# Prefix sums along the diagonal of four matrices: summing the upper part in one running row per partition, and loading the last full group row by row

## The chip, the cores and the metric

One core of one Trainium2 chip. The span is the time from the first to the last instruction in one profiled execution; it is about 1.7 us shorter than the time. TensorE is PE in the profile (PEld: its weight loads), VectorE is DVE, ScalarE is ACT, GpSimd is POOL, and SyncE, which issues the loads here, is SP.

## The reference

```python
B, H, W = 4, 4224, 4224
def reference(x):                       # x: fp32 [B, H, W]
    ps = np.cumsum(np.cumsum(x, axis=1), axis=2)
    diag = np.diagonal(ps, axis1=1, axis2=2)
    return np.cumsum(diag, axis=1).astype(np.float32)
```

Only the diagonal of the two-dimensional prefix sum is wanted, but every element of x has a part in it. So all of x, 285 MB, must be read once, and the output is 66 KB.

## The kernel before

Rows come in strips: a group is 384 rows, three per partition (F = 3), loaded whole as a [128, 3, 4224] tile (6336 KB) into one of three buffers. An image has 11 such groups. The step from diagonal element i-1 to i adds row i up to the diagonal and column i above it. So, per group, the kernel needs row sums to the left of the diagonal (ScalarE for 5/8 of the columns, VectorE for the rest; an instruction that sums a row also writes a by-product, a copy of what it summed: 128x2144 for 128x2144 in ScalarE's sums of group 8) and column sums to the right of it (VectorE adds the three rows of a partition, TensorE adds over the 128 partitions by multiplying with a selector). The block on the diagonal is split by a triangular mask.

```python
def add_up(strip, g, ws):                     # one group of 384 rows, before (shortened)
    k, hi = row_of(g), (g + 1) * GW
    mu = mup.tile([P, F, GW], FP32, name="mu")
    for q in range(F):
        act_sum(acc[:, k, q, 0:1], strip[:, q, :ws])             # ScalarE, writes a dump tile
    for q in range(F):
        masked(mu[:, q, :], strip[:, q, g*GW:hi], um3[:, q, :], acc[:, k, q, 2:3])
    for q in range(1, F):
        add_to(mu[:, 0, :], mu[:, q, :])
    columns(g, mu[:, 0, :], minus_sel)                           # TensorE
    if hi < N:
        for q in range(1, F):
            add_to(strip[:, 0, hi:], strip[:, q, hi:])
        for j in range(g + 1, NG):
            columns(j, strip[:, 0, j*GW:(j+1)*GW])               # TensorE, up to ten of them
    for q in range(F):
        pair_sum(acc[:, k, q, 1:2], strip[:, q, ws:hi])          # VectorE
```

The last image ends otherwise. Its group 10 comes in small pieces (called the last pieces below: two pieces of two thirds of the rows, five of the rest), and behind them stands a chain: row sums of d (`pu`), the carry between groups on TensorE, two scans, the weighing of the last sums, two small stores. Here d is the tile in which TensorE collects the steps along the diagonal (one row per group), and r3 are the row sums, which TensorE adds into d in six passes.

## Time and profile before

| | before |
|---|---|
| time, median of 3 (all of them) | 677.53 us (676.79 to 678.2) |
| span of the profiled execution | 675.7 us |
| busy: PE, DVE, ACT | 281.8, 387.9, 198.0 us |
| passes on PE, instructions on DVE | 576, 738 |
| read from memory | 285.47 MB |
| group 8 of the last image lands | 640.6 us |
| group 9 of the last image lands | 655.7 us |
| row sums of d (`pu`) start | 663.9 us |

How to read it: a landing is seen as the start of the first ScalarE operation on a strip, which waits for the load. The page's rows of tenths and of GB/s cut the span into 40 slices of 16.9 us; the timeline lists instructions in order with their start, their duration and, in brackets, the idle time before them and what ended it. The lines of both stand in the prediction.

### The profile page before, as it was taken

The page shows a single profiled execution, that of the slowest core. Times are in us where ns is not written, and L with a number is a line of the kernel's source. Part 1 is how long each engine was busy: PE and PEld are TensorE (multiplying, and loading weights), DVE is VectorE, ACT ScalarE, POOL GpSimd, SP SyncE. Part 2 cuts the span into 40 slices and gives each one's busy share as a digit, 9 for nine tenths or more (in the row PEclk, how much of TensorE's full clock was granted, in tenths as well). Part 3 has the DMA queues.
Part 4 walks back from the last instruction along what each step waited for, and adds up shares of the span by engine and source line. Part 5 has one row for each costly group of instructions (what it writes and reads, how often), then busy time and mean ns, then how long its engine had stood idle before and what let it go on. Part 6 is the DMA issues. An engine that isn't in the chain of part 4 may idle for free.

```text
span 675.7 us, 2520 instructions
## 1 busy us (share of the span) xinstructions
PE 281.8 (42%) x576; PEld 70.3 (10%) x576; DVE 387.9 (57%) x738; ACT 198.0 (29%) x275; POOL 7.1 (1%) x30
## 2 busy tenths in 40 slices
PE   0366455521037644532105545543212555663224
PEld 0021111100002111100001111100000111110002
DVE  1678666443377766444347776544445777554556
ACT  0121322334412122233451112223453111222446
POOL 4000000000000000000000000000000000000000
PEclk9977766665557777755556877775655687766666
DMA  9999999999999999999999999999999999999993
GB/s 384 432 419 433 432 432 433 438 439 430 432 432 432 435 436 432 433 432 432 432 435 432 432 433 431 432 432 432 432 432 436 432 432 433 432 432 430 435 400 128
DMA packets 7938, 285.69 MB, mean 423 GB/s; under 512 B 840, under 2 KB 1396, under 8 KB 2164
## 3 DMA queue, kind: packets, MB, share of 16 engines
q1 hardware_dynamic: 7924, 285.55, 98.2%
q8 instruction: 4, 0.07, 0.0%
q14 instruction: 10, 0.08, 0.0%
HBM read 285.47 MB, written 0.07 MB: 423 GB/s over the span
## 4 chain that ended last, share of the span: by engine, by line
DMA 72%; DVE 13%; PE 11%; ACT 2%; issue 1%; SPq 0%; DVEq 0%; ACTq 0%
DMA strip<-in_x_dram 72%; PE d L207 10%; DVE strip L236 8%; DVE mu L239 2%; ACT dump L214 2%; DVE mu L236 2%; PE fin_b L207 0%; DVE pair L225 0%; DVE c L377 0%; PE fin_a L207 0%; SPq L69 0%; DVE c L239 0%; DVE pu L219 0%; DVE yl L416 0%; DVE r L219 0%
## 5 line engine op out<-in xcount | busy, mean ns | idle before, releaser
L214 ACT ACTIVATE dump<-strip 128x224 bf16<-128x224 f32 (+13 forms) x137 | 184.0, 1343 | 453.4 <-DMA strip<-in_x_dram 450.4
L207 PE MATMUL d<-strip,sel 128*33 128x384 f32 (+1 forms) x440 | 223.3, 677 | 130.6 <-DVE strip L236 130.6
L239 DVE SCALAR_TENSOR_TENSOR mu<-strip,um 128x384 f32<-128x384 f32 x129 | 65.2, 555 | 265.0 <-DMA strip<-in_x_dram 265.0
L236 DVE TENSOR_TENSOR strip<-strip 128x3840 f32<-128x3840 f32 (+9 forms) x80 | 188.4, 2355 | 1.4
L207 PE MATMUL d<-mu,minus_sel 128*33 128x384 f32 (+1 forms) x86 | 51.9, 698 | 249.6 <-DVE mu L236 249.6
L207 PEld LDWEIGHTS d<-strip,sel 128*33 128x33 f32 (+1 forms) x440 | 58.2, 140 | 301.6 <-DVE strip L236 170.5
L225 DVE SCALAR_TENSOR_TENSOR pair<-strip 128x80 bf16<-128x80 f32 (+12 forms) x138 | 81.7, 592 | 3.2
L236 DVE TENSOR_TENSOR mu<-mu 128x384 f32<-128x384 f32 x86 | 47.8, 556 | 1.5
L207 PEld LDWEIGHTS d<-mu,minus_sel 128*33 128x33 f32 (+1 forms) x86 | 7.2, 122 | 283.9 <-DVE mu L236 280.9
L214 ACT ACTIVATION_READ_ACCUMULATOR dump<-strip 128x1 f32 x137 | 25.5, 186 | 0.0
L225 DVE DVE_READ_ACCUMULATOR pair<-strip 128x1 f32 x138 | 11.3, 82 | 0.0
L239 DVE DVE_READ_ACCUMULATOR mu<-strip,um 128x1 f32 x129 | 10.7, 83 | 0.0
L214 ACT ACT_TABLE_LOAD x1 | 1.3, 1283 | 19.1 <-DMA strip<-in_x_dram 19.1
L207 PE MATMUL d<-ones_all,r 128*33 128x128 f32 (+1 forms) x12 | 2.3, 346 | 5.9 <-DVE r L219 5.9
L200 DVE TENSOR_SCALAR steps<-steps 128x128 int32<-128x128 int32 x1 | 0.5, 461 | 5.8 <-POOL steps L199 5.8
L207 PE MATMUL fin_a<-weights,arows 128*1 128x256 f32 (+1 forms) x4 | 1.4, 513 | 3.1 <-DVE arows L219 3.1
L207 PEld LDWEIGHTS d<-ones_all,r 128*33 128x33 f32 (+1 forms) x12 | 1.4, 132 | 8.7 <-issue 5.3
L219 DVE TENSOR_REDUCE r<-acc 128x99 f32<-128x297 f32 (+1 forms) x2 | 0.7, 360 | 2.6 <-ACT dump L214 2.6
L207 PE MATMUL fin_b<-weights,bsum 128*1 128x128 f32 (+2 forms) x12 | 2.1, 364 | 0.0
L377 DVE TENSOR_TENSOR_SCAN c<-ones_all,carry,c 33x384 f32<-33x384 f32 (+1 forms) x2 | 2.0, 1008 | 0.1
L102 DVE MEMSET um<- 128x1152 bf16 (+1 forms) x2 | 1.4, 698 | 1.1 <-PEq L465 1.1
L377 DVE TENSOR_TENSOR_SCAN c<-ones_all,carry,d 33x384 f32<-33x384 f32 (+1 forms) x2 | 2.0, 1002 | 0.1
(62 smaller groups left out, 23.8 us busy)
## 6 DMA issues: line engine op xcount, KB each, us to landing
strip<-in_x_dram SPq DMA_DIRECT2D x43, 6336.0 KB, 32.1
strip<-in_x_dram SPq DMA_DIRECT2D x1, 2304.0 KB
strip<-in_x_dram SPq DMA_DIRECT2D x1, 1536.0 KB
strip<-in_x_dram SPq DMA_DIRECT2D x3, 480.0 KB, 31.4
head<-in_x_dram SPq DMA_DIRECT2D x1, 576.0 KB
strip<-in_x_dram SPq DMA_DIRECT2D x1, 352.0 KB, 32.0
strip<-in_x_dram SPq DMA_DIRECT2D x1, 128.0 KB, 24.7
out_dram<-c SPq DMA_DIRECT2D x1, 49.5 KB
```

What stands on the lines that cost most here:

```text
L102: nc.vector.memset(um, -1.0)
L200: nc.vector.tensor_single_scalar(out=steps, in_=steps, scalar=2, op=ALU.arith_shift_right)
L207: nc.tensor.matmul(o, lhsT=lhsT, rhs=rhs, start=start, stop=False, skip_group_check=True)
L214: nc.scalar.activation(out=dump[:, :w], in_=src, func=ACT.Copy, accum_out=acc)
L219: nc.vector.reduce_sum(out=acc, in_=src, axis=AX.X)
L225: nc.vector.scalar_tensor_tensor(out=pair[:, :w], in0=src[:, :w], scalar=1.0, in1=src[:, w:], op0=ALU.mult, op1=ALU.add, accum_out=acc,)
L236: nc.vector.tensor_add(out=o, in0=o, in1=i)
L239: nc.vector.scalar_tensor_tensor(out=o, in0=i, scalar=1.0, in1=m, op0=ALU.mult, op1=ALU.mult, accum_out=acc,)
L377: nc.vector.tensor_tensor_scan(out=c12[:, i, :], data0=ones_row[:rows], data1=src, initial=carry[:, i : i + 1], op0=ALU.mult, op1=ALU.add,)
```

## The change

The intent is to relieve TensorE and the start of each buffer's next load: VectorE adds everything on and above the diagonal up in one fp32 row u per partition, over all groups of an image, and TensorE reads a block of u once, when the group reaches it. ScalarE sums the full rows to the left, and writes its by-product into the strip itself instead of a dump tile. The head (the block on the diagonal of the last group) is loaded first, and group 9 of the last image is loaded and summed row by row.

```diff
-            add_up(strip, g, hi * 5 // 8 // 32 * 32)
+            for q in range(F):
+                act_sum(rsum[:, k, q : q + 1], strip[:, q, :hi])
+            block = strip[:, :, lo:hi]
+            nc.vector.tensor_mul(out=block, in0=block, in1=um3)
+            row_sums(rabove[:, k, :], block)
+            if g == 0:
+                nc.vector.tensor_add(out=u, in0=strip[:, 0, :], in1=strip[:, 1, :])
+                add_to(u, strip[:, 2, :])
+            else:
+                for q in range(F):
+                    add_to(u[:, lo:], strip[:, q, lo:])
+            columns(g, u_of(g))
 ... (in the last image, for g = 9)
+            for q in range(F):
+                load(out=strip[:, q, :], in_=rows_of(b, g)[:, q, :])
+            for q in range(F):
+                act_sum(rsum[:, k, q : q + 1], strip[:, q, :wa])         # wa = 2304
+                pair_sum(more[:, q : q + 1], strip[:, q, wa:hi])
+                block = strip[:, q, lo:hi]
+                masked(block, block, um3[:, q, :], rabove[:, k, q : q + 1])
+                add_to(u[:, lo:], strip[:, q, lo:])
+            for j in (g, LG):
+                columns(j, u_of(j))
+            add_to(rsum[:, k, :], more)
 ... (ScalarE's sum)
-        nc.scalar.activation(out=dump[:, :w], in_=src, func=ACT.Copy, accum_out=acc)
+        nc.scalar.activation(out=src, in_=src, func=ACT.Copy, accum_out=acc)
 ... (sums of the first of the last pieces: from before pu to after the carry's matmuls)
-            sum_a(1, *acuts[0], acuts[0][0] + 1536)
+        if not whole:
+            sum_a(1, *acuts[0], acuts[0][0] + 1536)
```

More of the change, by code (lines that the diff above doesn't have):

```diff
@@ L51 @@
     strips = ctx.enter_context(tc.tile_pool(name="strips", bufs=NBUF))
-    mup = ctx.enter_context(tc.tile_pool(name="mup", bufs=1))
     dumpool = ctx.enter_context(tc.tile_pool(name="dump", bufs=1))
@@ L63 @@
     ctx.enter_context(tc.manual_schedule())
-    def strip_tile():
-        return strips.tile([P, F, N], FP32, name="strip")
-    def load_rows(o, b, r0):
-        nc.sync.dma_start(
-            out=o, in_=x[b, r0 : r0 + GW, :].rearrange("(p f) w -> p f w", f=F)
-        )
-    prefetched = []
-    for i in range(NBUF):
-        t = strip_tile()
-        load_rows(t, 0, i * GW)
-        prefetched.append(t)
     NH = N - GW
@@ L85, with strip_tile, rows_of @@
     nc.sync.dma_start(out=head, in_=src[:, :, NH:N])
-    def selector(name, value):
-        t = consts.tile([P, 2 * NW - 1], FP32, name=name)
-        nc.vector.memset(t, 0.0)
-        nc.vector.memset(t[:, NW - 1 : NW], value)
-        return t
+    def strip_tile():
+        return strips.tile([P, F, N], FP32, name="strip")
+    def rows_of(b, g):
+        return x[b, g * GW : (g + 1) * GW, :].rearrange("(p f) w -> p f w", f=F)
+    load = nc.sync.dma_start
+    prefetched = []
+    for i in range(NBUF):
+        t = strip_tile()
+        load(out=t, in_=rows_of(0, i))
+        prefetched.append(t)
+    sel = consts.tile([P, 2 * NW - 1], FP32, name="sel")
+    nc.vector.memset(sel, 0.0)
+    nc.vector.memset(sel[:, NW - 1 : NW], 1.0)
     um3 = consts.tile([P, F, GW], BF16, name="um3")
@@ L98 @@
     for um, pattern, cm in (
+        (um1, [[1, GW]], -1),
         (um3, [[-1, F], [1, GW]], -F),
-        (um1, [[1, GW]], -1),
     ):
-        nc.vector.memset(um, -1.0)
+        nc.vector.memset(um, 1.0)
         nc.gpsimd.affine_select(
@@ L111 @@
         )
-    sel = selector("sel", 1.0)
-    minus_sel = selector("minus_sel", -1.0)
     ones_all = consts.tile([P, P + GW], FP32, name="ones_all")
@@ L211, in act_sum @@
     def act_sum(acc, src):
-        w = src.shape[-1]
-        dump = dumpool.tile([P, 2688], BF16, name="dump")
-        nc.scalar.activation(
-            out=dump[:, :w], in_=src, func=ACT.Copy, accum_out=acc
-        )
+        nc.scalar.activation(out=src, in_=src, func=ACT.Copy, accum_out=acc)
     def row_sums(acc, src):
@@ L223, in pair_sum @@
         w = src.shape[-1] // 2
-        pair = dumpool.tile([P, 1024], BF16, name="pair")
+        pair = dumpool.tile([P, 768], FP32, name="pair")
         nc.vector.scalar_tensor_tensor(
@@ L247, in masked @@
         )
-    accs = []
+    sums, above = [], []
     for i, n in enumerate((NW, NG)):
-        accs.append(consts.tile([P, n, F, 3], FP32, name=f"acc{i}"))
-        nc.gpsimd.memset(accs[i], 0.0)
+        for tiles, name in ((sums, "sums"), (above, "above")):
+            tiles.append(consts.tile([P, n, F], FP32, name=f"{name}{i}"))
+    for t in (sums[1], above[1]):
+        nc.vector.memset(t[:, 0, :], 0.0)
     asum = last.tile([P, 2, 5], FP32, name="asum")
@@ L260 @@
     hu = last.tile([P, 3], FP32, name="hu")
-    hmu = last.tile([P, F, GW], FP32, name="hmu")
-    def do_head():
-        row_sums(hs, head)
-        for h in range(F):
-            w = GW - h * P
-            masked(
-                hmu[:, h, GW - w :], head[:, h, GW - w :], um1[:, :w], hu[:, h : h + 1]
-            )
-        for h in range(1, F):
-            add_to(hmu[:, 0, h * P :], hmu[:, h, h * P :])
-        nc.vector.tensor_add(out=dtot, in0=hs, in1=hu)
-        nc.vector.tensor_copy(out=asum[:, :, 0], in_=dtot[:, 0:2])
+    row_sums(hs, head)
+    for h in range(F):
+        t = head[:, h, h * P :]
+        masked(t, t, um1[:, : GW - h * P], hu[:, h : h + 1])
+    for h in range(1, F):
+        add_to(head[:, 0, h * P :], head[:, h, h * P :])
+    nc.vector.tensor_sub(out=dtot, in0=hs, in1=hu)
+    nc.gpsimd.tensor_copy(out=asum[:, :, 0], in_=dtot[:, 0:2])
+    u = consts.tile([P, N], FP32, name="u")
     for b in range(B):
         whole = b < LB
-        acc = accs[b // LB]
         if b in (0, LB):
@@ L281, with columns, u_of @@
             first = [True]
+        rsum, rabove = sums[b // LB], above[b // LB]
         def row_of(j):
             return b * NG + j if whole else (j + 1) % NG
-        def columns(j, rhs, s=sel):
+        def columns(j, rhs):
             k = row_of(j)
-            matmul(d, s[:, NW - 1 - k : NW - 1 - k + rows], rhs, start=first[0])
+            matmul(d, sel[:, NW - 1 - k : NW - 1 - k + rows], rhs, start=first[0])
             first[0] = False
-        def add_up(strip, g, ws):
-            k = row_of(g)
-            hi = (g + 1) * GW
-            mu = mup.tile([P, F, GW], FP32, name="mu")
-            for q in range(F):
-                act_sum(acc[:, k, q, 0:1], strip[:, q, :ws])
-            for q in range(F):
-                block = strip[:, q, g * GW : hi]
-                masked(mu[:, q, :], block, um3[:, q, :], acc[:, k, q, 2:3])
-            for q in range(1, F):
-                add_to(mu[:, 0, :], mu[:, q, :])
-            columns(g, mu[:, 0, :], minus_sel)
-            if hi < N:
-                for q in range(1, F):
-                    add_to(strip[:, 0, hi:], strip[:, q, hi:])
-                for j in range(g + 1, NG):
-                    columns(j, strip[:, 0, j * GW : (j + 1) * GW])
-            for q in range(F):
-                pair_sum(acc[:, k, q, 1:2], strip[:, q, ws:hi])
-        for g in range(NG if whole else LG):
+        def u_of(j):
+            return u[:, j * GW : (j + 1) * GW]
+        for g in range(NG if whole else LG - 1):
             strip = prefetched.pop(0) if prefetched else None
@@ L316 @@
                 strip = strip_tile()
-                load_rows(strip, b, g * GW)
-            hi = (g + 1) * GW
-            add_up(strip, g, hi * 5 // 8 // 32 * 32)
-            if b == 0 and g == NBUF - 1:
-                do_head()
-            if not whole and g == 1:
-                columns(LG, hmu[:, 0, :], minus_sel)
+                load(out=strip, in_=rows_of(b, g))
+            k, lo, hi = row_of(g), g * GW, (g + 1) * GW
+            for q in range(F):
[11 more added lines that the diff above has]
+        if not whole:
+            columns(LG, head[:, 0, :])
+            g = LG - 1
+            k, lo, hi = row_of(g), g * GW, LG * GW
+            strip = strip_tile()
+            more = last.tile([P, F], FP32, name="more")
+            wa = 2304
+            for q in range(F):
[9 more added lines that the diff above has]
+            add_to(rsum[:, k, :], more)
         if b < LB - 1:
@@ L327 @@
         r3 = last.tile([P, rows, F], FP32, name=f"r3_{rows}")
-        row_sums(r3, acc)
+        nc.vector.tensor_sub(out=r3, in0=rsum, in1=rabove)
         for q in range(F):
@@ L338 @@
             for c0, c1 in acuts:
-                nc.sync.dma_start(out=part_a[:, :, c0:c1], in_=src_a[:, :, c0:c1])
+                load(out=part_a[:, :, c0:c1], in_=src_a[:, :, c0:c1])
             CB = NH // 4
@@ L349 @@
                 r0 = TB + sb * R
-                nc.sync.dma_start(
+                load(
                     out=part_b[:, sb, c0:c1],
@@ L373 @@
         matmul(carry_ps[:, 1:2], apart, pu[:, 0:1])
+        if not whole:
+            sum_a(1, *acuts[0], acuts[0][0] + 1536)
         carry = last.tile([rows, 2], FP32, name=f"carry{rows}")
```

## The prediction

> **What bounds the kernel now.** I read the page first, then the chain that ended last, then the timeline of the last 70 us, then windows and the DMA view. The page:
>
> ```profile
> GB/s 384 432 419 433 432 432 433 438 439 430 432 432 432 435 436 432 433 432 432 432 435 432 432 433 431 432 432 432 432 432 436 432 432 433 432 432 430 435 400 128
> ...
> HBM read 285.47 MB, written 0.07 MB: 423 GB/s over the span
> ...
> DMA 72%; DVE 13%; PE 11%; ACT 2%; issue 1%; SPq 0%; DVEq 0%; ACTq 0%
> ```
>
> The loads run at 432 GB/s nearly throughout, while DVE is busy for 57%, PE for 42% and ACT for 29% of the span. 285.47 MB at 432 GB/s take 661 of the 675.7 us. The change moves the same bytes, so only some 15 us (2.2%) lie outside the stream: the first latency and the tail. The DVE and PE shares of the chain are no cost of their own: the chain passes through the release of a buffer, but the stream has no hole there. So the question is the tail, and when its strips land. Its timeline (start and duration in us):
>
> ```profile
> 640.62 1.99 ACT L214 ACTIVATE dump<-strip 128x2144 bf16<-128x2144 f32 x1 [9.25 <-DMA strip<-in_x_dram]
> ...
> 655.68 2.20 ACT L214 ACTIVATE dump<-strip 128x2400 bf16<-128x2400 f32 x1 [8.75 <-DMA strip<-in_x_dram]
> ...
> 661.15 0.91 DVE L225 SCALAR_TENSOR_TENSOR pair<-strip 128x720 bf16<-128x720 f32 x1
> ...
> 663.91 0.54 DVE L219 TENSOR_REDUCE pu<-d 11x1 f32<-11x384 f32 x1
> ...
> 671.64 0.29 DVE L225 SCALAR_TENSOR_TENSOR pair<-strip 128x128 bf16<-128x128 f32 x1
> ```
>
> The last two full strips (groups 8 and 9 of the last image) land at 640.6 and 655.7. From 655.7 on VectorE and ScalarE are nearly solid: group 9 is summed by 662.4, the row sums of d (pu) start at 663.91, and from there it is 11.8 us to the end, nearly all VectorE. Beside this the end of the stream, in windows (last two columns: DMA share, GB/s):
>
> ```profile
> 663.00:664.00 1.00, 0.80 (x6) 0.46 (x6) 0.96 (x5) 1.00 (x1) 0.00 (x0) 1.00 0.65 245
> 664.00:665.00 1.00, 0.00 (x0) 0.00 (x0) 0.92 (x3) 0.97 (x3) 0.00 (x0) 0.78 0.27 98
> 665.00:670.00 5.00, 1.80 (x10) 0.62 (x11) 4.08 (x12) 4.81 (x13) 0.00 (x0) 0.50 0.07 27
> ```
>
> 27 GB/s is 432/16: from 665 to 669.5 one DMA engine alone still works. Most were done at 664; one lags by some 5 us, and a strip counts as landed only when the slowest has done its part. Where does the lag come from? The first ScalarE operation of each strip shows strips landing every 15.0 us, except for gaps of 15.8 to 16.0 that end at 171.9, 292.9, 413.8, 519.7 and 625.6 (and 16.9 at 66.0, with the head's load in it). Each of these windows, and few others, holds a packet of instructions; the DMA view of the window 609.7 to 625.6:
>
> ```profile
> q1 hardware_dynamic: 149, 6.74, 98.4%
> q14 instruction: 1, 0.01, 0.1%
> ```
>
> They lie about 120 us apart. VectorE issues 738 instructions in 676 us, some 130 in 120 us[...]. So I take them for VectorE's own instruction fetches: six, each delaying one DMA engine by about 0.97 us.
>
> [...] The trace has 390 at 224 columns and 2390 at 2624[...]; start to start 2.32 us at 2400, so I use 0.32 us + 0.833 ns each. [...]
>
> **The change, part by part.**
> TensorE: 288 matmuls (576 passes on the page) become 69, as the order of instructions lists them: per group one 384-column matmul of u in place of up to eleven. 281.8 us of PE become about 65. None of it sets the stream; it only leaves the release of a strip.
> ScalarE: the row sums take all columns to the diagonal instead of 5/8 of them: per image 3 x (0.833 x 384 x 66 + 11 x 320) ns = 74 us, about 290 us in all (198 before).
> VectorE: per strip one product over 1152 columns (1.36), one reduction (1.35, the head's 128x1152 took 1347 ns), three adds to u of the strip's width, in place of three masked products, four adds and three pair sums. Widest: group 1, 2.7 + 3 x 4.16 = 15.2 us; group 0 11.8; group 10 4.4. Per image some 110 us, in all about 450 us (388 before).
> New wait: ScalarE now writes the strip itself, up to the block on the diagonal, so VectorE's product starts only after all three of ScalarE's sums (the order of instructions lists that wait). Life of a strip after landing: group 1, 2.9 + 15.2 = 18.1 us; group 5, 6.7 + 10.4 = 17.1; group 10, 11.5 + 4.4 = 15.9. Before it was 19.1 us for the first strip (landed 19.17, reload issued 38.27). Three buffers give 45.0 us per round; the first strip shows 18.4 us from issue to landing on an empty queue, so a life up to 26.6 us is hidden. The stream keeps its rate.
>
> The tail, first with the old landing times:
> 1. Group 8 lands at 640.6. ScalarE: 3 x (0.32 + 2.88) = 9.6, to 650.2. VectorE idles until then (group 7 was done at 642), then 1.36 + 1.35 + 3 x 1.37 = 6.8, to 657.0.
> 2. Group 9 comes row by row, landing near 645.6, 650.6, 655.6, but VectorE is free only at 657.0: all three rows are there, the split buys it nothing. Per row pair sum 1.04, masked product 0.56, add of 768 columns 0.96: 2.5 to 2.6 us, three rows to 664.6. Before: 662.0.
> 3. The last u lets TensorE run four passes at the half clock (before, four took 2.61), then six passes for r3, about 1.2 (before 0.83, at full clock): pu starts at 668.5 instead of 663.9. VectorE idles over 3 us.
> 4. From pu to the end 11.8 as before, plus the two pair sums now put after the masked product, 1.15, less the wait for carry that they fill, 0.42: 12.5. End at 681.0: **5.3 us later**.
> ScalarE ends group 9 at 658 and is off the path.
>
> The lag, second: VectorE's issued instructions fall from 738 to about 300[...]; TensorE's fall by three quarters. With three or four fetches less, groups 8 and 9 land about **3.5 us earlier**, and steps 1 to 4 shift with them. Sum: 675.7 + 5.3 - 3.5 = 677.5 us of span; the time is 1.8 above the span (677.5 against 675.7): **679.4 us**, 0.3% slower.
>
> **The rivals.**
> A. The tail is saved, as intended: row by row loading and fewer TensorE operations take some 3 us off, and the lag 3.5 more: 671 us. For it: group 9's ScalarE sums end 4 us earlier. Against it: VectorE, not ScalarE, would be last, since it must first wait out group 8's sums.
> B. The fetches cost nothing (the gaps have another cause, and stay): then only the longer tail shows, 683 us.[...] Against it: six coincidences.
> C. The serial ScalarE-then-VectorE life of a strip starves the queue, so VectorE becomes the bound in groups 1 to 3 (15.2 us against 15.0): if a life passed 26.6 us, several us per image, 690 or more. Against it: 18 us, and group 0 and groups 3 to 10 give slack back.
> None reaches 2% (13.6 us) easily: faster would need 664, just above the stream's 661 with no tail at all.
>
> **Range and chances.** Between A in part and B: 675.5 to 683.5. The time before spreads by 1.4 us. Same within 2%: 0.97; slower 0.02 (C); faster 0.01.
>
> **What would show it.** Stream at 432 GB/s in all middle slices and strips 15.0 us apart, with about two long gaps instead of six (else B, or C where the rate falls). PE busy near 65, ACT near 290, DVE near 450 us. Group 8's product starting 9.6 us after its landing; VectorE reaching group 9's last row after its landing; an idle of about 3 us before pu on TensorE; pu to end 12.5 us. The single DMA engine's lone stretch after 664 shrinking from 5 to about 2 us. If VectorE waits for a row's landing in group 9, or pu starts within 8.5 us of group 9's last landing (12.9 here), step 1 or 2 is wrong.

The sum is 675.7 + 5.3 - 3.5 = 677.5 us of span, 679.4 us of time. The adds of fp32 columns took 4155 ns at 3840 columns, 1755 at 1536 and 1355 at 1152 in the kernel before (hence the 4.16 of the widest strip and the 1.36 and 1.37 of group 8). The 390 and 2390 are ns of one of its sums on ScalarE, at 224 and 2624 columns: 0.833 ns a column. The 3.5 us are an estimate: six gaps for 738 instructions are one for every 123, so about 300 instructions would have two or three; three or four fewer, at 0.97 us each, are 2.9 to 3.9 us.

The half and the full clock of step 3 (the half clock is also named in the expectation of run 4) are read in the kernel before: its records grant 0.50 over the four passes from 658.33 to 661.07 (1.46 and 1.49 us for two), 0.55 over the four that took 2.61, and 1.00 over the six that took 0.83. That a strip has landed only with the slowest engine's part is seen at the end of the changed kernel: the last of ScalarE's operations to wait for a load starts at 665.43, and the lone engine (26 GB/s from 665 to 665.5) is done by 665.5.

## More of the kernel before

The time is the device time of one execution in microseconds (us), taken as the median of several executions.

A span quoted here is that of one execution; spans of one kernel lie up to 1.7 us apart within one set of runs, so a small difference of two spans says little.

## The result, and the profile after

The changed kernel takes 678.15 us (median of 4, 677.55 to 678.29) against 677.75 (median of 4) in the same rounds: ratio 1.0006, 95% interval 0.9989 to 1.0023. That is the same within noise. Ratios here are the mean time of one kernel's runs over that of the other's of the same rounds, so not quite the ratio of the quoted medians.

The page of the changed kernel, the rows that answer to those of before:

```profile
GB/s 373 438 435 435 438 435 435 435 435 432 435 435 432 432 438 432 432 432 432 432 432 432 432 432 432 429 432 432 435 432 432 432 432 432 432 432 429 426 417 93
```

The stream is what it was, and so is the span, although the engines' work has changed places altogether:

```profile
PE 74.3 (11%) x138; PEld 13.1 (2%) x138; DVE 448.9 (66%) x277; ACT 276.2 (41%) x275; POOL 6.9 (1%) x29
...
q14 instruction: 7, 0.06, 0.0%
q8 instruction: 1, 0.02, 0.0%
...
DMA 54%; DVE 27%; ACT 15%; issue 2%; PE 2%; SPq 0%; ACTq 0%; DVEq 0%
```

207 us of TensorE's busy time are gone, and not a microsecond of the time with them. VectorE has 61 us more to do, with 277 instructions instead of 738. The packets of instructions fell from 14 to 8. The chain that ended last now runs through VectorE and ScalarE (a buffer is released by VectorE, which has waited for ScalarE), which before were 13% and 2% of it; as the rate shows, this costs the stream nothing.

The timeline of the changed kernel's tail (start and duration in us):

```profile
636.45 3.08 ACT L211 ACTIVATE strip<-strip 128x3456 f32<-128x3456 f32 x1 [6.65 <-DMA strip<-in_x_dram]
...
645.79 1.36 DVE L297 TENSOR_TENSOR strip<-strip,um 128x1152 f32<-128x1152 f32 x1 [7.96 <-ACT strip L211]
...
651.55 2.12 ACT L211 ACTIVATE strip<-strip 128x2304 f32<-128x2304 f32 x1 [1.57 <-DMA strip<-in_x_dram]
...
652.51 0.95 DVE L220 SCALAR_TENSOR_TENSOR pair<-strip 128x768 f32<-128x768 f32 x1
...
660.05 2.73 PE L205 MATMUL d<-u,sel 128*11 128x384 f32 x4 [4.67 <-DVE u L231]
...
664.11 0.55 DVE L214 TENSOR_REDUCE pu<-d 11x1 f32<-11x384 f32 x1 [3.80 <-PE d L205]
...
672.45 0.29 DVE L220 SCALAR_TENSOR_TENSOR pair<-strip 128x128 f32<-128x128 f32 x1
```

Group 8 lands 4.2 us earlier than before (636.45 against 640.62), and the row sums of d start as late as before (664.11 against 663.91). What lies between: VectorE idles 8 us for ScalarE's sums of group 8 (645.79), starts group 9 at 652.51, when its last row (651.55) is already there, and idles 3.8 us more for TensorE before `pu`. The end of the stream, in windows (last two columns DMA share and GB/s; the third figure from the end is PE's clock):

```profile
663.00:664.00 1.00, 1.00 (x6) 0.43 (x3) 0.00 (x0) 0.93 (x4) 0.00 (x0) 1.00 0.39 143
664.00:665.00 1.00, 0.07 (x1) 0.00 (x0) 0.89 (x2) 0.54 (x3) 0.00 (x0) 1.00 0.16 58
665.00:666.00 1.00, 0.54 (x6) 0.25 (x6) 0.97 (x5) 0.69 (x4) 0.00 (x0) 1.00 0.04 13
```

The lone last DMA engine is done by 665.5, where before it worked on to 669.5. So the arithmetic of the tail closes: landing of group 8, 4.17 us earlier; from there to `pu`, 27.66 us instead of 23.29 (4.37 more); from `pu` to the end, 12.5 instead of 11.8. Sum: 0.9 us later, the difference of the spans (676.6 against 675.7) of these two executions; the other three of the changed kernel have 675.8 to 676.4.

### The profile page after: what moved, and what is told of

It reads as the page before. It is cut to its first block, busy times and chain, and to the rows that moved or that the text cites. A ratio compares the mean times of both kernels' runs of the same rounds, so it can differ in the third digit from the quotient of the medians.

```text
span 676.6 us, 1096 instructions
## 1 busy us (share of the span) xinstructions
PE 74.3 (11%) x138; PEld 13.1 (2%) x138; DVE 448.9 (66%) x277; ACT 276.2 (41%) x275; POOL 6.9 (1%) x29
## 4 chain that ended last, share of the span: by engine, by line
DMA 54%; DVE 27%; ACT 15%; issue 2%; PE 2%; SPq 0%; ACTq 0%; DVEq 0%
DMA strip<-in_x_dram 54%; DVE u L231 16%; ACT strip L211 15%; DVE strip L297 4%; DVE above L214 4%; DVE u L300 2%; PE d L205 1%; DVE pair L220 1%; DVE c L379 0%; PE fin_b L205 0%; DVE strip L234 0%; PE fin_a L205 0%; DVE pu L214 0%; DVE c L234 0%; ACTq L211 0%
## 5 line engine op out<-in xcount | busy, mean ns | idle before, releaser
L211 ACT ACTIVATE strip<-strip 128x768 f32<-128x768 f32 (+11 forms) x137 | 270.5, 1975 | 388.9 <-DMA strip<-in_x_dram 362.3
L231 DVE TENSOR_TENSOR u<-u,strip 128x3840 f32<-128x3840 f32 (+10 forms) x121 | 299.1, 2472 | 2.9
L297 DVE TENSOR_TENSOR strip<-strip,um 128x1152 f32<-128x1152 f32 x42 | 57.0, 1357 | 204.1 <-ACT strip L211 204.1
L205 PE MATMUL d<-u,sel 128*33 128x384 f32 (+1 forms) x88 | 65.0, 844 | 593.7 <-DVE u L231 593.7
L214 DVE TENSOR_REDUCE above<-strip 128x3 f32<-128x1152 f32 x42 | 56.8, 1353 | 1.5
L211 ACT ACTIVATION_READ_ACCUMULATOR strip<-strip 128x1 f32 x137 | 25.5, 186 | 0.0
L205 PEld LDWEIGHTS d<-u,sel 128*33 128x33 f32 (+1 forms) x88 | 7.6, 134 | 648.5 <-DVE u L231 647.5
L300 DVE TENSOR_TENSOR u<-strip 128x4224 f32<-128x4224 f32 x4 | 18.2, 4548 | 0.0
L220 DVE SCALAR_TENSOR_TENSOR pair<-strip 128x384 f32<-128x384 f32 (+5 forms) x12 | 6.9, 577 | 0.2
L234 DVE SCALAR_TENSOR_TENSOR strip<-strip,um 128x384 f32<-128x384 f32 x3 | 1.7, 557 | 0.1
```

Of the source, the lines that this page charges most:

```text
L205: nc.tensor.matmul(o, lhsT=lhsT, rhs=rhs, start=start, stop=False, skip_group_check=True)
L211: nc.scalar.activation(out=src, in_=src, func=ACT.Copy, accum_out=acc)
L214: nc.vector.reduce_sum(out=acc, in_=src, axis=AX.X)
L220: nc.vector.scalar_tensor_tensor(out=pair[:, :w], in0=src[:, :w], scalar=1.0, in1=src[:, w:], op0=ALU.mult, op1=ALU.add, accum_out=acc,)
L231: nc.vector.tensor_add(out=o, in0=o, in1=i)
L234: nc.vector.scalar_tensor_tensor(out=o, in0=i, scalar=1.0, in1=m, op0=ALU.mult, op1=ALU.mult, accum_out=acc,)
```

## The experiments

Theory: the stream sets the time up to the last landings; VectorE's fetches of its instructions delay one DMA engine and with it every landing, so that fewer VectorE instructions bring the landings forward; the tail then gives this back, because VectorE waits for ScalarE's in-place sums and then for TensorE. The main rivals: the gaps between landings have nothing to do with fetches; the row by row load is what counts in the tail; TensorE's relief counts. All runs gave correct results; each was compared with the kernel before, run on the same chip in the same rounds (median 677.53 to 677.73 us). Where a run is set beside the changed kernel, two sets of rounds on different chips are compared, by their spans and landings.

**1. More VectorE instructions (681.44 us, ratio 1.0061, 1.0047 to 1.0075).**

```diff
             columns(g, u_of(g))
+            if whole or g < LG - 3:
+                for i in range(11):              # a spare tile, another element each time
+                    nc.vector.memset(idle[0:1, c : c + 1], 0.0)
```

> The changed kernel with eleven one-element memsets on VectorE (some 60 ns each) after each of the first 40 strips, so that VectorE issues about 717 instructions (738 in the kernel before, 277 in the changed one). None in the last two strips, so the tail's own work is as in the changed kernel. Theory (VectorE's instruction fetches delay one DMA engine by about 0.97 us each): five or six long gaps between landings instead of two, group 8 of the last image lands near 640 us instead of 636.5, the whole tail shifts with it, and the span grows by 3 to 4 us to about 680. Rival B (the fetches cost nothing; the gaps had another cause): landing at 636.5 and span 676.6, both within 0.5 us.

VectorE issued 717 instructions, but was busy only 5.6 us longer in all (454.5 us), 12.7 ns a memset (the expected 60 are near the 59 ns that a 128x1 memset took in the kernel before). Gaps of 15.9 to 16.0 us instead of 15.0 ended at 65.7, 186.6, 292.6, 413.5, 519.4 and 625.3: six again, though the head's load no longer lies in the first one. Group 8:

```profile
640.34 3.08 ACT L211 ACTIVATE strip<-strip 128x3456 f32<-128x3456 f32 x1 [6.68 <-DMA strip<-in_x_dram]
```

3.9 us later than in the changed kernel, four gaps of 0.97 us, and the span grew by 3.9 to 680.5. The count of VectorE instructions moves the landings: rival B, in which the gaps have another cause and stay, is out. That it does so by its fetches is read from the packets: the DMA view of each of the six gaps holds one of q14. But three more windows between landings hold one too (those that end at 155.7, 443.5 and 579.4) and are 15.0 us long, so that a packet does not always put a landing off. Whose these are the trace does not say. That a single DMA engine lags is seen at the end: at 27 GB/s, a sixteenth of 432, it works on alone until past 669, in the changed kernel until 665.5.

**2. The same padding on GpSimd (678.86 us, ratio 1.0019, 1.0007 to 1.0032).** The same edit with `nc.gpsimd.memset`.

> The same eleven memsets per strip, on GpSimd instead of VectorE, as a control for VectorE's time. If what counts is the fetches, whichever engine makes them, some four more packets of instructions appear and group 8 lands 2 to 4 us later than 636.5, span 679 to 680; if GpSimd's fetches go through a DMA engine that is not the slowest one, they are partly hidden and the landing moves by less than 2 us. If instead VectorE's being busier is what delays landings, nothing moves here: 636.5 and 676.6 within 0.5 us.

Not the test that it was meant to be: GpSimd waits for nothing here, so it ran through all of its memsets between 14.9 and 32.3 us (in lots of 128 at most, the last three with pauses of 2.02 us between them), and its four extra packets of instructions came at once. The second strip lands late:

```profile
20.26 0.52 ACT L211 ACTIVATE strip<-strip 128x384 f32<-128x384 f32 x1 [18.16 <-DMA strip<-in_x_dram]
37.41 0.84 ACT L211 ACTIVATE strip<-strip 128x768 f32<-128x768 f32 x1 [15.53 <-DMA strip<-in_x_dram]
```

17.15 us apart instead of 15.0, with VectorE no busier than in the changed kernel (449.0 us). But group 8 landed at 637.02, only 0.6 us late, and the two gaps that the changed kernel has at 140.7 and 456.5 are gone. A reading that fits: GpSimd's fetches delayed another DMA engine by 2.2 to 2.4 us, and a landing waits for the slowest engine, so the two delays do not add but hide one another. That they were on different DMA engines was argued from this, not seen; the trace does not name the DMA engine of a packet.

**3. Group 9 in one load (678.04 us, ratio 1.0008, 0.9995 to 1.002).**

```diff
-            for q in range(F):
-                load(out=strip[:, q, :], in_=rows_of(b, g)[:, q, :])
+            load(out=strip, in_=rows_of(b, g))
```

> The changed kernel with group 9 loaded by one transfer instead of three, its row-wise sums unchanged. Theory (VectorE is busy with group 8 until 652.5, when all rows have landed at 651.55, so the split of the load buys nothing): VectorE ends group 9 at 659.9 and the span is 676.6, within 0.4 us. Rival (the row by row loading pays): VectorE's last row ends up to 5 us later, span 679 or more.

Span 676.3 against 676.6; VectorE began group 9 at 652.29 and ended its last add at 659.7. In the changed kernel the split of the load buys nothing.

**4. Group 8 summed row by row too (672.27 us, ratio 0.9923, 0.9911 to 0.9936).**

```diff
-        for g in range(NG if whole else LG - 1):
+        for g in range(NG if whole else LG - 2):
 ...
+            for g in (LG - 2, LG - 1):           # the row by row sums, for groups 8 and 9;
 ...                                             # 8 is still loaded whole
```

> The changed kernel with group 8 of the last image also summed row by row in the manner of group 9 (ScalarE takes columns up to 2304, VectorE a pair sum of the rest), loaded whole. ScalarE then does not write what VectorE needs, so VectorE has no wait for ScalarE. Theory (the wait for ScalarE's in-place sums is what makes the tail late): VectorE starts group 8 at its landing, 636.5, ends it by 645, takes group 9's rows as they land, ends them at 654.3 instead of 659.9, row sums of d start at 658.5 instead of 664.1, and the span falls by 5 to 6 us, to about 671, where the last landing (665.5) begins to bind. Rival (the tail is bound by the last landings or by TensorE's half clock): the span falls by less than 2 us.

```profile
636.50 2.12 ACT L211 ACTIVATE strip<-strip 128x2304 f32<-128x2304 f32 x1 [6.64 <-DMA strip<-in_x_dram]
...
637.80 0.75 DVE L220 SCALAR_TENSOR_TENSOR pair<-strip 128x576 f32<-128x576 f32 x1
...
651.59 0.96 DVE L220 SCALAR_TENSOR_TENSOR pair<-strip 128x768 f32<-128x768 f32 x1 [0.68 <-DMA strip<-in_x_dram]
...
658.26 0.55 DVE L214 TENSOR_REDUCE pu<-d 11x1 f32<-11x384 f32 x1 [3.80 <-PE d L205]
```

VectorE no longer waits for ScalarE on group 8: it starts at 637.80, when it is done with group 7 (636.5 was expected), and then it does wait for a row's landing (651.59). `pu` starts 5.85 us earlier, at 658.26, and the span is 670.2. The wait for ScalarE's sums of one strip was what cost the tail its gain. That ScalarE's in-place write is what makes VectorE wait was not tested alone: VectorE's product is also written in place, on the block that ScalarE's sums read to their end, and by the code that alone would make it wait with a dump tile too. The edit took both away, since ScalarE's sums now stop short of the block. The edit also moves 3 x 1152 columns of sums from ScalarE to VectorE; that this is not what helps is plain from VectorE's work on the strip, which grew, from 6.8 to 8.1 us.

**5. Two pair sums back before `pu` (677.18 us, ratio 0.9994, 0.9981 to 1.0006).** The last part of the diff, undone.

> The changed kernel with one of its reorderings undone: the two pair sums of the first piece of the last rows stand before the row sums of d again, as in the kernel before. Step 4 of the prediction counted their move as 1.15 us added less 0.42 us of a wait that they fill, 0.7 us. VectorE idles 3.8 us before the row sums (664.1), so put there the pair sums cost nothing: row sums still at 664.1, then a wait of about 0.5 us for the carry, span 0.5 to 0.7 us shorter, 675.9 to 676.1. Rival (their data lands too late, or VectorE is not the bound there): no change, or later.

`pu` 663.85 and span 675.4, with group 8 landing 0.25 us earlier than in the changed kernel (636.20). Less that 0.25, a gain of 0.9 us of span, from one execution of each; all five of this run (spans 675.3 to 675.6) lie below all four of the changed kernel (675.8 to 676.6). VectorE had idle time before `pu`; the wait for the carry was 0.42 us.

**6. TensorE kept busy before the last matmuls (676.39 us, ratio 0.9981, 0.9969 to 0.9994).**

```diff
+            for i in range(4):
+                matmul(warm, sel[:, :rows], head[:, 0, :], start=True)
             columns(LG, head[:, 0, :])
```

> The changed kernel with four dummy matmuls of 384 columns on TensorE, into a spare tile, right before the head's matmul of the last image (652.6), so that TensorE is busy for some 7 us up to the last matmuls. Theory (an idle TensorE works at half pace): the four passes of u at 660.0 take about 1.4 us instead of 2.73 and the six of r3 0.83 instead of 1.49, the row sums of d start at 662.2 instead of 664.1, and the span falls by 1.9 us to 674.7. Rival (the pace has another cause, as the clock of the changed kernel's records, 0.995, would have it): passes unchanged at 0.64 us each, span 676.6 within 0.4 us.

```profile
660.04 1.46 PE L205 MATMUL d<-u,sel 128*11 128x384 f32 x4 [1.75 <-DVE u L231]
...
661.34 0.82 PE L205 MATMUL d<-ones_all,r 128*11 128x128 f32 x6
...
662.20 0.55 DVE L214 TENSOR_REDUCE pu<-d 11x1 f32<-11x384 f32 x1 [1.90 <-PE d L205]
```

The same four passes take 1.46 us instead of 2.73 and the same six 0.82 instead of 1.49, and the span falls by 1.9 us to 674.7. So TensorE's pace hung on what it did before: the four passes are slow after 4.67 us of idling and fast after 1.75 us behind the dummy work, and within that work the pace doubles, from a weight load every 0.64 us (up to 655.80) to one every 0.32 to 0.33 (from 656.19). How long it must idle or work for that was not tested. The granted clock in the records does not show the two paces here: it is 1.00 over 660 to 663.9 of the changed kernel, while the four passes took 2.73 us, and its mean is 0.995 in both runs. Set beside the kernel before, only r3 is slower in the changed one (0.83 us before, 1.49 now): the four passes of group 9 were slow there too (1.46 and 1.49 us for two), but VectorE's pair sums ran at the same time. What is new is that all ten now stand between VectorE's last add and `pu`.

**7. TensorE's work put back (677.94 us, ratio 1.0005, 0.9992 to 1.0019).** Five dummy matmuls after each of the first 40 strips.

> The changed kernel with five dummy matmuls after each of the first 40 strips, so that TensorE has 400 passes more (538, against 576 before) and is busy for some 280 to 330 us again; nothing waits for them. Theory (TensorE's work was never on the path, so taking it away saved nothing by itself): stream at 432 GB/s, span within 0.5 us, except for TensorE's own instruction fetches, some three more packets of 16 KB, which may make another DMA engine the slowest and move the landing of group 8 from 636.5 by up to 2 us. Rival (TensorE's load counts by itself, by holding buffers): landings late by more than 3 us.

```profile
PE 256.8 (38%) x538; PEld 70.6 (10%) x538; DVE 448.9 (66%) x277; ACT 276.3 (41%) x275; POOL 6.9 (1%) x29
...
q8 instruction: 4, 0.07, 0.0%
```

Group 8 landed at 636.33, the span was 675.9. TensorE's work moved neither. Its three more packets of some 16 KB (four on q8 are 0.07 MB) did move landings on the way: the window that ends at 306.35 is 15.19 us long and holds one packet of q8 and no other (14.98 in the changed kernel, without one), and the one that ends at 156.23 is 15.64 us long, with one of q8 and one of q14. But the next long gap, at 456.41, is then 15.13 instead of 15.97, and at group 8 nothing is left of them. It is as in run 2: delays hide one another, which fits delays on different DMA engines.

**8. The row by row part alone, in the kernel before (676.03 us, ratio 0.9975, 0.9963 to 0.9988).** Three loads for group 9 and its operations ordered by row; ScalarE's dump tile stays.

> The kernel before with one part of the change alone: group 9 of the last image loaded in three transfers and summed row by row, everything else as before (ScalarE writes to a tile of its own, so VectorE has no wait for it). Landings as in the kernel before (group 8 at 640.6, last row at 655.7). VectorE ends the last row at 658.4 instead of 662.0, ScalarE at 658 instead of 662.4; four passes on TensorE then stand behind the last row, so that the row sums of d start at about 662.5 instead of 663.9: span 674.3, 1.4 us shorter, not the full 4. Rival A (the row by row part is worth its 3 to 4 us): span 672 to 672.7.

`pu` started at 662.52 instead of 663.91, span 674.4. VectorE was through with the last row 2.3 us after its landing, but TensorE's passes (two of mu, two of the strip, six of r3, each lot about 1.5 us, done at 661.75) then stood behind it, and last of all came VectorE's two pair sums, which waited for a landing until 661.44 and ended as `pu` started. So the expected 662.5 was met, but the landing held `pu` longer than the passes that were expected to. Alone, this part is worth 1.3 us of span.

**9. Group 8 by rows, the pair sums early, and four dummies (671.40 us, ratio 0.9907, 0.989 to 0.9923).**

> The changed kernel with the three edits that helped together: group 8 summed row by row as well, the two pair sums before the row sums of d, four dummy matmuls ahead of the head's. Separately they gave 6.4, 1.2 and 1.9 us of span. They cannot add up: with group 8 by rows alone the last pieces land at 665.4 and the end at 670.2 is 4.8 us after that, of which the last two pair sums, the last matmuls and the store take over 4. Theory (the last landing binds now): span 669.2 to 670.0, time 671.0 to 672. Rival (the edits add up): span 667 or less.

Span 670.0. One of the three did nothing: with group 8 by rows the head's matmul stands before group 8, so that its dummies ran at 639, and the four passes of u at 654.01 took 2.73 us again. And the end was not the last landing alone:

```profile
665.23 2.13 PE L205 MATMUL fin_b<-weights,bsum 128*1 128x128 f32 x12
```

TensorE, back at the slow pace (2.13 us for these twelve passes, 1.15 in run 10), closed the chain. So the expected number came out of a reason that was only half right.

**10. Group 8 by rows, and five dummies before the last products (670.99 us, ratio 0.9906, 0.989 to 0.9923).**

> The kernel of the run with group 8 by rows, plus five dummy matmuls on TensorE between the carry's matmuls (659.5) and the last products. The run with all three edits had its dummy matmuls in a useless place (the head's matmul had moved ahead of group 8, so they ran some 13 us before they were wanted, and the four passes of u still took 2.73 us), and its end waited on TensorE's last products at half pace (twelve passes, 2.13 us). Here the five should take some 4.5 us, to 664, and the last products then run at full pace: fin_a 0.8 us instead of 1.44, the twelve passes 1.5 or less. Theory (the end is now the last landing, 665.4, plus short work): span 669.2 to 669.7 against 670.2. Rival (the dummies stand in the way of the first product at 663.9): span 670.2 or more.

```profile
659.34 3.40 PE L205 MATMUL warm<-head,sel 128*11 128x384 f32 x10
...
663.66 0.81 PE L205 MATMUL fin_a<-weights,arows 128*1 128x256 f32 x4 [0.70 <-DVE arows L214]
...
664.74 1.15 PE L205 MATMUL fin_b<-weights,bsum 128*1 128x128 f32 x12
665.27 0.44 ACT L211 ACTIVATE strip<-strip 128x288 f32<-128x288 f32 x1 [0.28 <-DMA strip<-in_x_dram]
```

The span of the profiled execution is 668.6, but it is the shortest of four: the others have 669.2 to 669.4, as expected. In it the last landing (665.27) now is 3.3 us before the end, of which two pair sums, the last products and a store are the rest. This is the fastest kernel, 1% below both kernels; runs 9 and 10 cannot be told apart (the intervals coincide, and run 9's spans are 669.4 to 670.0).

## Why the prediction was right

It said 679.4 us, 675.5 to 683.5, and the same within 2%; it was 678.15. That the time stays within 2% was hardly a test of the mechanism: by its own words no rival reached 2% easily. What tests it are the terms (in spans): 5.3 us lost in the tail, 5.1 measured (4.37 and 0.7), and 3.5 won by earlier landings, 4.2 measured. (Its last sum has a slip: 677.5 and 1.8 are 679.3.)

- **The stream keeps its rate.** Right: 429 to 438 GB/s in the middle slices. The lives of the strips that it worked out never starved the queue, and rival C did not appear.
- **Work by engine.** PE 74.3 us (said near 65), ACT 276.2 (290), DVE 448.9 (450). PE's term was low: the 138 passes took 0.54 us each, where the kernel before had 0.49 (281.8 over 576). Nearly all of them now ran at the slow pace, two of u in 1.45 to 1.49 us. The work that was taken off was not on the path, as run 7 shows; the last ten passes are (run 6).
- **Fetches.** Right in kind: run 1 brought the six gaps back and the landings with them. The size was a little low: group 8 landed 4.2 us earlier, 3.5 was said. Two gaps were left (they end at 140.7 and 456.5), four fewer, which by run 1 are worth 3.9 us. (Six gaps for 738 instructions are one for every 123, in run 1 six for 717. The ten packets on q14 in the kernel before are 0.08 MB, so 8 KB each.) The other 0.3 us is what still separates run 1 from the kernel before (640.34 against 640.62); the head's load, which now comes ahead of the first strip instead of between strips, may be the cause, but no run tests it. Two readings were too strong: that "few others" of the windows hold a packet (in the kernel before five of 15.0 to 15.2 us do, such as that which ends at 111.16), and that strips land 15.0 us apart whatever VectorE does: with 440 memsets more (run 1) six gaps are 15.9 to 16.0.
- **Step 1,** the wait for ScalarE's sums of group 8: 9.3 us from landing to VectorE's start against 9.6, and run 4 shows it to be the largest term that can be taken away.
- **Step 2,** the split load buys nothing: run 3. VectorE reached group 9 after its last landing, as said.
- **Step 3,** the idle before `pu`: 3.8 us, said "over 3". Run 6 shows its cause: with the passes in 1.46 and 0.82 us instead of 2.73 and 1.49 it is 1.9 us.
- **Step 4,** `pu` to the end: 12.5 us, as said; the move of the two pair sums was counted at 0.7 and measured at 0.9 (run 5).
- **Rival A** (the tail is saved) lost because of the order of work on VectorE, not because its gain is unreal: with the wait out of the way (run 4) the time is 672.27, near its 671.

So where did the expected gain go? TensorE's relief was never on the path. The earlier landings, 4.2 us, which come from the shorter list of VectorE's instructions (3.9) and from something that was not isolated (0.3), were given back by the new wait of VectorE for ScalarE on group 8 and by TensorE's passes, at the slow pace (2.73 and 1.49 us), behind VectorE's last add. What stays open: which DMA engine serves whose fetches, and which of the two in-place writes makes VectorE wait.

## What to carry to other kernels

Where a load stream bounds a kernel, look at its last landing and at the order of work behind it; 207 us of busy time elsewhere were worth nothing here. Two engines that work in place on the same columns of a strip form a chain (VectorE stood idle for 7.96 us before group 8's product), which the buffers hid in the middle of this stream and nothing hid at its end (5.85 us in run 4), so give them different columns in the last strips. And where loads wait for the slowest DMA engine, the number of instructions can itself be a cost: here 3.9 us of span for 440 memsets (run 1).
